# A HGRN2 mixer whose key products, sums and logarithms are placed anew on VectorE and ScalarE

## The chip, the cores and the metric

The kernel runs on one core of one Trainium2 chip. It computes one inference step of a small hybrid network (four layers; 512 noisy tokens and 128 context tokens) in one launch. The metric is the device time in microseconds, a median over runs. Engines are called TensorE (PE in the rows), VectorE (DVE), ScalarE (ACT), GpSimd (POOL) and SyncE (SP, which only starts DMAs here).

## The reference, cut to what matters

Four layers follow each other: differential attention, retention, HGRN2, differential attention. Each normalises its input, multiplies it with an input matrix, mixes the tokens, and multiplies with an output matrix. The change touches the HGRN2 layer alone. Its core, for each of 8 heads and for both directions:

```python
def gates(fl, lbd):
    f = lbd + (1.0 - lbd) * jax.nn.sigmoid(fl)
    return jnp.log(f), 1.0 - f                      # log decay g, key k

def step(S, inp):                                    # one chunk of 64 tokens
    qc, kc, vc, gc = inp
    b = lax.cumsum(gc, axis=1)
    ref = b[:, mid:mid + 1]
    sc = einsum(qc * exp(b - ref), kc * exp(ref - b)) * causal
    o = sc @ vc + (qc * exp(b)) @ S
    b_last = b[:, -1:]
    S = exp(b_last) * S + (kc * exp(b_last - b)).T @ vc
    return S, o

of, sf = gla_scan(q, kf, i, gf, s0[:, 0])
ob, sb = gla_scan(q[:, ::-1], kb[:, ::-1], i[:, ::-1], gb[:, ::-1], s0[:, 1])
o = rms_norm(of + ob[:, ::-1], norm_g)
y = (o * silu(g)) @ w_out
```

## The kernel before, in words

All tokens (640: 512 and 128) stand on the free axis; a head's 128 key channels are the partitions. Weights arrive in pieces of 512 KB. ScalarE copies each piece to a rounded type (`whi`, L178) and VectorE takes the rest (`wlo`, L116), so that three matmuls per product give full precision. A matmul group of the input projection is therefore three lines: L250 to L252 (one head's column of 128 outputs, 320 tokens at a time) or L225 to L227 (256 columns of values or of the output gate).

The HGRN2 layer (`hg`, L1056) first projects head 0 (`hg_proj`) and then, for each head h, weaves two generators: `hg_mix` of head h, the main one, and `hg_proj` of head h+1 as fill (for the last head the start of the output layer, `tail`). `hg_mix` yields numbers where TensorE would wait (6.0, 1.5, 6.0, 1.5, 4.0, 4.0), and `weave` issues as much fill as each number, scaled, asks for. This decides the order on TensorE, which is written by hand: it runs its instructions exactly in the order of issue. On the other engines the order is set by a scheduler, from the order of issue and its own estimate of times; there each engine too runs its queue strictly in order.

`hg_proj` of a head computes, in succession, a value or gate block (`iv` or `sg`, by the parity of the head; none for head 7), then three columns: the query `q`, the forward gate `th0`, the backward gate `th1`. Each column comes in two halves, and each half ends with a tanh on ScalarE (L1143). When a column is done, its weight buffers are handed to the next piece, so that a weight copy (L178) on ScalarE stands directly behind the column.

`hg_mix` does for each direction d: key `k` (VectorE), logarithm `g` (ScalarE, L1174, which needs another activation table than tanh and exp), running sum `c` (VectorE scan, L1177 or L1180), the difference `dd` to a reference, its exponentials `e1`, `e2` (L1186, L1187), the products `qd` (VectorE) and `kd` (GpSimd), the difference `xx` and its exponentials (L1197, L1198) with the half-size products `of` (two a direction), the exponential of `c` (L1204) with `qe` and `dl`, the distance `ll` to the block's end on GpSimd, its exponential (L1211), and the product `ke` on GpSimd. Then come four transposes of `ke` on TensorE (L1218), their copy `kt` on ScalarE (L1220), the state products (L1224), and VectorE's updates of the state (L1228). After both directions follow the score products (L1243 to L1247), masks, a sum on GpSimd (L1254), and the output products (L1259 to L1262). All products go through one helper line, L1155. The temporaries (`w0`, shown as `w`) rotate through five buffers.

Of the kernel before, what the change touches and what calls it, by code (L numbers as in the profile page):

```python
# [11 lines left out]
F32 = mybir.dt.float32  # L12
# [3 lines left out]
AF = mybir.ActivationFunctionType  # L16
ALU = mybir.AluOpType
# [4 lines left out]
P = 128  # L22
# [66 lines left out]
class Net:  # L89
# [966 lines left out]
    def hg(self, l, y):  # L1056
        nc, tc, t = self.nc, self.tc, self.t
        with tc.tile_pool(name=f"hg{l}", bufs=1, reuse_waits="tile") as mp:
            rs = self.const(mp, "rs")
            mf = mp.tile([P, NT, 64], U8, name="mf")  # L1060
            mg = mp.tile([P, NT, 64], U8, name="mg")
            for m, n in ((mf, "mf"), (mg, "mg")):
                c = mp.tile([P, 640], F32, tag="w0", bufs=5, name="w0")[:, 0:320]
                nc.sync.dma_start(c, t["consts"][:, CWHERE[n][0]:sum(CWHERE[n])])
                nc.vector.tensor_copy(m.rearrange("p a b -> p (a b)"), c)
            self.gain = self.gains[:, 0:1]

            tt_ = nc.vector.tensor_tensor
            mx = mp.tile([P, 2, 8], F32, name="lmx")
            ex = mp.tile([P, 2, 4, 8], F32, name="lex")  # L1070
            su = mp.tile([P, 2, 8], F32, name="lsu")
            tt_(out=mx, in0=self.lbl[:, :, 0, :], in1=self.lbl[:, :, 1, :], op=ALU.max)
            for i in (2, 3):
                tt_(out=mx, in0=mx, in1=self.lbl[:, :, i, :], op=ALU.max)
            tt_(out=ex, in0=self.lbl, in1=mx.unsqueeze(2).to_broadcast([P, 2, 4, 8]), op=ALU.subtract)
            nc.scalar.activation(ex, ex, AF.Exp)
            tt_(out=su, in0=ex[:, :, 0, :], in1=ex[:, :, 1, :], op=ALU.add)
            for i in (2, 3):
                tt_(out=su, in0=su, in1=ex[:, :, i, :], op=ALU.add)
            nc.vector.reciprocal(su, su)  # L1080
            tt_(out=ex, in0=ex, in1=su.unsqueeze(2).to_broadcast([P, 2, 4, 8]), op=ALU.mult)
            lb = mp.tile([P, 2, 8], F32, name="lb")
            tt_(out=lb, in0=ex[:, :, 0, :], in1=ex[:, :, 1, :], op=ALU.add)
            for i in range(2, l + 1):
                tt_(out=lb, in0=lb, in1=ex[:, :, i, :], op=ALU.add)
            tt_(out=lb, in0=lb, in1=ex[:, :, 0, :], op=ALU.subtract)
            co = mp.tile([P, 3, 2, 8], F32, name="lco")
            for i, (a, b) in enumerate(((-0.5, 0.5), (0.5, 0.5), (0.5, -0.5))):
                nc.vector.tensor_scalar(out=co[:, i], in0=lb, scalar1=a, scalar2=b, op0=ALU.mult, op1=ALU.add)
            pz = [mp.tile([P, NT, 64], F32, name=f"z{d}") for d in range(2)]  # L1090
            for z in pz:
                nc.vector.memset(z, 0.0)
            st = types.SimpleNamespace(mp=mp, l=l, rs=rs, mf=mf, mg=mg, co=co, pz=pz, iv={}, sg={}, h={})
            for _ in self.hg_proj(st, 0):
                pass
            for h in range(HEADS):
                if h < 7:
                    self.weave(self.hg_mix(st, h, y), self.hg_proj(st, h + 1), 24.0, 30.0 if h < 6 else 18.0)
                else:
                    self.weave(self.hg_mix(st, h, y), self.tail(l, y, 2), 24.0, 12.0)  # L1100

    def hg_proj(self, st, h):
        nc, t, mp = self.nc, self.t, st.mp
        if h == 0:
# [3 lines left out]
            def use(tt, ps):  # L1108
                nc.scalar.activation(iv[:, tt, :], ps[:, 0, :], AF.Copy)
                self.gate(sg[:, tt:tt + 1, :], ps[:, 1:2, :])  # L1110
# [11 lines left out]
        hd = st.h[h] = types.SimpleNamespace(th=[])  # L1122

        def halves(ps, j):
            return ((slice(j * 256, j * 256 + 256), samples(ps, j)), (slice(NS + j * 64, NS + j * 64 + 64), prompts(ps, j)))
# [11 lines left out]
        for d in range(2):  # L1137
            th = mp.tile([P, 640], F32, tag=f"th{d}", bufs=2, name="th")
            hd.th.append(th)

            def use(j, ps):
                for c, u in halves(ps, j):
                    nc.scalar.activation(th[:, c], u, AF.Tanh, scale=0.5)  # L1143

            yield from self.proj_b(st.l, 1024 + d * 1024 + h * 128, use)

    def hg_mix(self, st, h, y):
        nc, t, mp = self.nc, self.t, st.mp
        p, m = h // 2, h % 2
        iv, sg, rs, mf, mg, co, pz = st.iv[p], st.sg[p], st.rs, st.mf, st.mg, st.co, st.pz  # L1150
# [2 lines left out]
        ch = lambda a: a.rearrange("p (c i) -> p c i", i=64)  # L1153
        bl = lambda a: a.rearrange("p (c i) -> p c i", i=128)
        TT = lambda eng, o, a, b, op: eng.tensor_tensor(out=o, in0=a, in1=b, op=op)  # L1155
        DV, PL = nc.vector, nc.gpsimd

        def tmp():
            return mp.tile([P, 640], F32, tag="w0", bufs=5, name="w0")

        def lin(tag, n=640, bufs=1):
            return mp.tile([P, n], F32, tag=tag, bufs=bufs, name=tag)

        s32 = mp.tile([P, 8, P], F32, tag="s32", name="s32")
        for d in range(2):
            nc.sync.dma_start(s32[:, 4 * d, :], t["state_hgrn"][0, 0, d, h])
        res = []
        for d in range(2):
            th = st.h[h].th[d]
            hs, hb, nhs = (co[:, i, d, h:h + 1] for i in range(3))  # L1170
            k = lin(f"k{d}")
            DV.tensor_scalar(out=k, in0=th, scalar1=nhs, scalar2=hs, op0=ALU.mult, op1=ALU.add)
            g = tmp()
            nc.scalar.activation(g, th, AF.Ln, scale=hs, bias=hb)  # L1174
            c = lin(f"c{d}")
            if d == 0:
                DV.tensor_tensor_scan(c, rs, g, 0.0, op0=ALU.mult, op1=ALU.add)  # L1177
                ref, mid, last = 32, 63, 127
            else:
                DV.tensor_tensor_scan(c[:, ::-1], rs, g[:, ::-1], 0.0, op0=ALU.mult, op1=ALU.add)  # L1180
                ref, mid, last = 31, 64, 0

            dd = tmp()
            TT(DV, ch(dd), ch(c), ch(c)[:, :, ref:ref + 1].to_broadcast([P, 10, 64]), ALU.subtract)
            e1, e2 = tmp(), tmp()
            nc.scalar.activation(e1, dd, AF.Exp)  # L1186
            nc.scalar.activation(e2, dd, AF.Exp, scale=-1.0)  # L1187
            qd, kd = lin(f"qd{d}"), lin(f"kd{d}")
            TT(DV, qd, q, e1, ALU.mult)
            TT(PL, kd, k, e2, ALU.mult)  # L1190

            xx = tmp()
            TT(DV, bl(xx), bl(c), bl(c)[:, :, mid:mid + 1].to_broadcast([P, 5, P]), ALU.subtract)
# [12 lines left out]
            TT(DV, qe, q[:, 0:NS], ec_[:, 0:NS], ALU.mult)  # L1206
            dl = lin(f"dl{d}", 5)
            DV.tensor_copy(dl, bl(ec_)[:, :, last])
            ll = tmp()
            TT(PL, bl(ll), bl(c)[:, :, last:last + 1].to_broadcast([P, 5, P]), bl(c), ALU.subtract)  # L1210
            nc.scalar.activation(ll, ll, AF.Exp)  # L1211
            ke = tmp()
            TT(PL, ke, k, ll, ALU.mult)
            yield 6.0
            pt = self.one([P, 4, P])
            blocks = (0, 1, 2, 4) if d == 0 else (1, 2, 3, 4)
            for i, b in enumerate(blocks):
                nc.tensor.transpose(pt[:, i, :], bl(ke)[:, b, :], self.ident)  # L1218
            kt = mp.tile([P, 4, P], F32, tag=f"kt{d}", name="kt")
# [6 lines left out]
            for n, i in enumerate(order):  # L1226
                b = blocks[i]
# [21 lines left out]
        f2, g2 = pz  # L1249
        DV.copy_predicated(f2, mf, fd)  # L1250
        DV.copy_predicated(g2, mg, gp)
        p1 = bl(tmp())
        for s, u in ((A, B), (B, A)):
            TT(PL, p1[s, :, s], f2[s], g2[s], ALU.add)  # L1254
            nc.scalar.activation(p1[s, :, u], fo[s], AF.Copy)
        yield 4.0
        o = self.two([P, 8, P])
# [180 lines left out]
```

## Time and profile before

| | |
|---|---|
| median of 3 runs | 1885.02 us (1884.73 to 1887.43) |
| the profiled execution's own time | 1885.44 us |
| its span | 1883.7 us |
| busy: TensorE, weight load, VectorE, ScalarE, GpSimd | 96%, 88%, 69%, 52%, 16% |
| mean granted TensorE clock | 0.989 of full speed |
| the HGRN2 heads | about 1086 to 1420 us of the span |

The span is the time between the first and last recorded instruction; the device time lies 1.7 us above it. A busy share of TensorE is an average over four layers. The heads of the HGRN2 layer follow each other at about 43 us: the forward logarithms of heads 0, 3 and 7 start at 1087.9, 1216.2 and 1380.8 us.

### The profile page before, as it was taken

The numbers are of one execution on the slowest core, as the hardware profiler recorded it, in microseconds if no ns is written. First come the engines' busy times: TensorE is split into PE (matmuls) and PEld (weight loads), VectorE is DVE, ScalarE is ACT, GpSimd is POOL, SyncE is SP. The second block draws the span as 40 slices with busy tenths as digits, with TensorE's granted clock in tenths as the row PEclk, the third lists the DMA queues.
The fourth block names the chain that finished last, engine by engine and source line by source line (L and its number), as shares of the span: only waits on it lengthen the run. The fifth ranks groups of instructions, "written<-read, shape, count | busy, mean of one in ns | idle before, by whom it ended". The sixth has DMA issues, their size and how long they took to land.

```text
span 1883.7 us, 31931 instructions
## 1 busy us (share of the span) xinstructions
PE 1804.6 (96%) x12060; PEld 1650.3 (88%) x12060; DVE 1304.6 (69%) x2681; ACT 980.7 (52%) x2271; POOL 300.2 (16%) x249
## 2 busy tenths in 40 slices
PE   5999999999999999999999999999989999999998
PEld 3889999977888889889878899999978889999976
DVE  4878888847788898873335566666774776767654
ACT  3556676655544434443333366666664545655552
POOL 0000000003222223222101222332331200000001
PEclk9999999999999999999999999999989999999999
DMA  9644555414454445343323222222214463443322
GB/s 302 187 127 139 148 151 167 119 49 154 122 164 149 135 151 157 124 135 101 116 92 101 86 69 74 65 63 74 62 41 137 139 170 90 114 115 101 98 73 101
DMA packets 231536, 224.39 MB, mean 119 GB/s; under 512 B 11619, under 2 KB 201558, under 8 KB 231382
## 3 DMA queue, kind: packets, MB, share of 16 engines
q1 hardware_dynamic: 230912, 221.96, 39.3%
q8 instruction: 95, 1.56, 0.3%
q14 instruction: 59, 0.48, 0.1%
q10 hardware_dynamic: 470, 0.39, 0.1%
HBM read 174.59 MB, written 18.35 MB: 102 GB/s over the span
## 4 chain that ended last, share of the span: by engine, by line
PE 66%; DVE 15%; ACT 7%; DMA 5%; issue 3%; SPq 2%; POOL 1%; DVEq 0%; ACTq 0%; POOLq 0%
PE one L470 7%; PE one L472 7%; PE one L471 7%; PE one L250 5%; PE one L251 5%; PE one L252 5%; PE one L225 3%; PE one L826 3%; PE one L226 3%; PE one L227 3%; DVE macc L367 3%; DVE wlo L116 2%; PE two L788 2%; PE two L789 2%; PE one L816 1%
## 5 line engine op out<-in xcount | busy, mean ns | idle before, releaser
L250 PE MATMUL one<-hh,whi 128*128 128x320 f32 x1152 | 364.8, 317 | 3.9 <-DVE modT L339 1.6
L252 PE MATMUL one<-hh,wlo 128*128 128x320 f32 x1152 | 356.4, 309 | 0.3 <-DVE wlo L116 0.3
L251 PE MATMUL one<-hl,whi 128*128 128x320 f32 x1152 | 356.4, 309 | 0.0
L116 DVE TENSOR_TENSOR wlo<-raw,whi 128x1024 fp32r<-128x1024 f32 x192 | 235.9, 1234 | 143.9 <-ACT whi L178 143.2
L470 PE MATMUL one<-whi,hh 128*128 128x512 f32 x744 | 301.8, 406 | 6.8 <-ACT yo L565 3.5
L472 PE MATMUL one<-whi,hl 128*128 128x512 f32 x744 | 294.6, 396 | 0.4 <-DVE hl L444 0.4
L471 PE MATMUL one<-wlo,hh 128*128 128x512 f32 x744 | 292.9, 394 | 0.0
L178 ACT ACTIVATE whi<-raw 128x1024 fp32r<-128x1024 f32 x192 | 201.5, 1056 | 152.8 <-PE one L251 58.6
L250 PEld LDWEIGHTS one<-hh,whi 128*128 128x128 f32 x1152 | 217.3, 189 | 6.0 <-DVE modT L339 2.0
L251 PEld LDWEIGHTS one<-hl,whi 128*128 128x128 f32 x1152 | 217.4, 189 | 0.5
L252 PEld LDWEIGHTS one<-hh,wlo 128*128 128x128 f32 x1152 | 217.2, 189 | 0.5 <-DVE wlo L116 0.5
L367 DVE SCALAR_TENSOR_TENSOR macc<-mraw,smod,macc 128x256 f32<-128x256 f32 x432 | 209.1, 527 | 1.3 <-DMA mraw<-in_w_mod 1.1
L397 POOL TENSOR_TENSOR rs<-ms,mhalf 128x1 f32<-128x1 f32 (+1 forms) x72 | 65.7, 913 | 897.6 <-DVE ms L395 724.4
L225 PE MATMUL one<-whi,hh 128*128 128x256 f32 x720 | 207.7, 289 | 0.0
L226 PE MATMUL one<-wlo,hh 128*128 128x256 f32 x720 | 201.0, 279 | 0.0
L227 PE MATMUL one<-whi,hl 128*128 128x256 f32 x720 | 200.9, 279 | 0.0
L470 PEld LDWEIGHTS one<-whi,hh 128*128 128x128 f32 x744 | 141.6, 190 | 37.2 <-ACT yo L565 3.9
L472 PEld LDWEIGHTS one<-whi,hl 128*128 128x128 f32 x744 | 141.0, 190 | 34.5 <-DVE hl L444 1.3
L471 PEld LDWEIGHTS one<-wlo,hh 128*128 128x128 f32 x744 | 141.5, 190 | 27.7
L225 PEld LDWEIGHTS one<-whi,hh 128*128 128x128 f32 x720 | 135.4, 188 | 1.5
L226 PEld LDWEIGHTS one<-wlo,hh 128*128 128x128 f32 x720 | 135.6, 188 | 0.0
L227 PEld LDWEIGHTS one<-whi,hl 128*128 128x128 f32 x720 | 135.1, 188 | 0.0
(345 smaller groups left out, 3540.1 us busy)
## 6 DMA issues: line engine op xcount, KB each, us to landing
mraw<-in_w_mod SPq DMA_DIRECT2D x96, 512.0 KB, 4.1
raw<-in_da_w_in SPq DMA_DIRECT2D x56, 512.0 KB, 4.5
raw<-in_hg_w_in SPq DMA_DIRECT2D x36, 512.0 KB, 3.9
raw<-in_ret_w_in SPq DMA_DIRECT2D x64, 256.0 KB, 3.0
kk<-ks SPq DMA_DIRECT2D x64, 160.0 KB, 2.9
kz<-ks SPq DMA_DIRECT2D x64, 160.0 KB, 2.8
qq<-q SPq DMA_DIRECT2D x64, 128.0 KB, 3.0
raw<-in_da_w_out SPq DMA_DIRECT2D x16, 512.0 KB, 3.9
```

The lines of the kernel that those rows point to most:

```text
L116: return (eng or self.nc.gpsimd).tensor_tensor(out=out, in0=full, in1=hi.bitcast(F32), op=ALU.subtract)
L178: self.nc.scalar.activation(hi, raw, AF.Copy)
L225: mm(out, xh, wh[:, k % 4, :], start=(first and k == ks[0]), stop=False)
L226: mm(out, xh, wl[:, k % 4, :], start=False, stop=False)
L227: mm(out, xl, wh[:, k % 4, :], start=False, stop=(last and k == ks[-1]))
L250: nc.tensor.matmul(ps, wh[:, k, :], self.hh[:, k, c], start=(k == 0), stop=False)
L251: nc.tensor.matmul(ps, wh[:, k, :], self.hl[:, k, c], start=False, stop=False)
L252: nc.tensor.matmul(ps, wl[:, k, :], self.hh[:, k, c], start=False, stop=(k == KT - 1))
L367: nc.vector.scalar_tensor_tensor(out=m, in0=raw[:, k, :], scalar=c, in1=m, op0=ALU.mult, op1=ALU.add)
L470: mm(ps, xh, wh, start=(first and k == ks[0]), stop=False)
L471: mm(ps, xh, wl, start=False, stop=False)
L472: mm(ps, xl, wh, start=False, stop=(last and k == ks[-1]))
```

## The change

Five edits, all in `hg_mix` but for one handle:
- both directions' logarithms are issued in succession, and made to stand behind the last tanh of the head's projection (`issue_after`);
- `kd`, `ke` and the sums of L1254 move from GpSimd to VectorE;
- the distance `ll` is no longer computed: the exponential takes `c` with scale -1 and the block's last value as its bias, one instruction for each of the four blocks that are needed;
- the product `ke` is made for the needed blocks alone (384 + 128 columns forward, 512 backward);
- the temporaries rotate through six buffers (also where the masks are loaded, L1063).

```diff
@@ hg_proj
-                    nc.scalar.activation(th[:, c], u, AF.Tanh, scale=0.5)
+                    hd.last = nc.scalar.activation(th[:, c], u, AF.Tanh, scale=0.5)
@@ hg_mix
-            return mp.tile([P, 640], F32, tag="w0", bufs=5, name="w0")
+            return mp.tile([P, 640], F32, tag="w0", bufs=6, name="w0")
-        res = []
+        res, gs = [], [tmp(), tmp()]
+        with self.tc.issue_after(st.h[h].last.ins):
+            for d in range(2):
+                nc.scalar.activation(gs[d], st.h[h].th[d], AF.Ln, scale=co[:, 0, d, h:h + 1], bias=co[:, 1, d, h:h + 1])
         for d in range(2):
-            th = st.h[h].th[d]
-            hs, hb, nhs = (co[:, i, d, h:h + 1] for i in range(3))
+            th, g = st.h[h].th[d], gs[d]
+            hs, nhs = co[:, 0, d, h:h + 1], co[:, 2, d, h:h + 1]
-            g = tmp()
-            nc.scalar.activation(g, th, AF.Ln, scale=hs, bias=hb)
...
-            TT(PL, kd, k, e2, ALU.mult)
+            TT(DV, kd, k, e2, ALU.mult)
...
-            ll = tmp()
-            TT(PL, bl(ll), bl(c)[:, :, last:last + 1].to_broadcast([P, 5, P]), bl(c), ALU.subtract)
-            nc.scalar.activation(ll, ll, AF.Exp)
+            blocks = (0, 1, 2, 4) if d == 0 else (1, 2, 3, 4)
             ke = tmp()
-            TT(PL, ke, k, ll, ALU.mult)
+            for b in blocks:
+                nc.scalar.activation(bl(ke)[:, b, :], bl(c)[:, b, :], AF.Exp, scale=-1.0, bias=bl(c)[:, b, last:last + 1])
+            for bs in (slice(0, 3), slice(4, 5)) if d == 0 else (slice(1, 5),):
+                TT(DV, bl(ke)[:, bs, :], bl(ke)[:, bs, :], bl(k)[:, bs, :], ALU.mult)
...
-            TT(PL, p1[s, :, s], f2[s], g2[s], ALU.add)
+            TT(DV, p1[s, :, s], f2[s], g2[s], ALU.add)
```

On TensorE and on SyncE the instructions and their order are the same before and after (line numbers behind the edits are one higher). GpSimd keeps one small instruction a head in this layer. ScalarE and VectorE are ordered anew.

ScalarE before, head 3, from the forward gate's last tanh on (`th` are the gates, `w` with a number a temporary, `hsq` the squares of head 2's output):

```order
L178 ACTIVATE whi<-raw 128x1024
L1143 ACTIVATE th<-one 128x256
L1143 ACTIVATE th<-one 128x64
L1174 ACT_TABLE_LOAD
L1174 ACTIVATE w_13052<-th,lco 128x640
L1143 ACT_TABLE_LOAD
L1143 ACTIVATE th<-one 128x256
L1143 ACTIVATE th<-one 128x64
L1186 ACTIVATE w_13058<-w_13056 128x640
L1187 ACTIVATE w_13059<-w_13056 128x640
```

And the same place after, where the `th` rows are the backward gate's two halves:

```order
L1143 ACTIVATE th<-one 128x256
L1143 ACTIVATE th<-one 128x64
L649 ACTIVATE hsq,hss<-two 128x128 x5
L178 ACTIVATE whi<-raw 128x1024
L1143 ACTIVATE th<-one 128x256
L1143 ACTIVATE th<-one 128x64
L1170 ACT_TABLE_LOAD
L1170 ACTIVATE w_13059<-th,lco 128x640
L1170 ACTIVATE w_13060<-th,lco 128x640
L1187 ACT_TABLE_LOAD
L1187 ACTIVATE w_13069<-w_13067 128x640
L1188 ACTIVATE w_13070<-w_13067 128x640
```

The forward logarithm stood behind the forward gate, with the backward gate's tanh behind it; now both logarithms stand behind the backward gate's second half, with one table load ahead of them and one behind.

VectorE before, head 3, from the forward scan on (`c` the running sum, the two `w` the differences `dd` and `xx`; the forward `ke` was GpSimd's):

```order
L1177 SCALAR_TENSOR_TENSOR c_13054<-c_rs,w_13052 128x640
L1155 TENSOR_TENSOR w_13056<-c_13054 128x640
L1155 TENSOR_TENSOR w_13066<-c_13054 128x640
L1155 TENSOR_TENSOR qd_13062<-q,w_13058 128x640
L1155 TENSOR_TENSOR of_13071<-k_13050,w_13068 128x5x64
L1155 TENSOR_TENSOR of_13071<-q,w_13068 128x5x64
L1155 TENSOR_TENSOR qe_13076<-q,w_13074 128x512
L1208 COPY dl_13078<-w_13074 128x5
```

And after, from the forward scan to the forward `ke` (`w_13091`, the last row of its two):

```order
L1178 SCALAR_TENSOR_TENSOR c_13065<-c_rs,w_13059 128x640
L1181 SCALAR_TENSOR_TENSOR c_13219<-c_rs,w_13060 128x640
L1155 TENSOR_TENSOR w_13067<-c_13065 128x640
L1155 TENSOR_TENSOR w_13077<-c_13065 128x640
L1155 TENSOR_TENSOR qd_13073<-q,w_13069 128x640
L1155 TENSOR_TENSOR kd_13074<-k_13063,w_13070 128x640
L1155 TENSOR_TENSOR w_13221<-c_13219 128x640
L632 SCALAR_TENSOR_TENSOR sg<-sg,one 128x512
L1155 TENSOR_TENSOR of_13082<-k_13063,w_13079 128x5x64
L1155 TENSOR_TENSOR qe_13087<-q,w_13085 128x512
L1155 TENSOR_TENSOR w_13091<-w_13091,k_13063 128x384
L1155 TENSOR_TENSOR w_13091<-w_13091,k_13063 128x128
```

Ahead of the forward `ke` now stand the other direction's scan and difference, `kd`, and the `ke` products themselves. In heads 0, 2 and 4 there is no `sg` row here; the backward direction's second difference stands ahead of `ke` in its place.

## Rows read from the trace of the kernel before

**Rows 1.** Busy by stretch: length, PE, PEld, DVE, ACT, POOL, granted PE clock, DMA, GB/s.
```profile
1085.00:1130.00 45.00, 43.39 (x372) 42.98 (x371) 29.31 (x38) 28.56 (x49) 11.17 (x8) 1.00 0.21 63
...
1210.00:1250.00 40.00, 39.89 (x355) 39.50 (x354) 28.03 (x42) 26.27 (x51) 10.87 (x7) 1.00 0.20 58
...
1330.00:1370.00 40.00, 36.72 (x308) 36.00 (x307) 27.10 (x45) 26.11 (x55) 12.98 (x9) 1.00 0.23 67
1370.00:1420.00 50.00, 42.93 (x348) 38.63 (x347) 31.19 (x52) 29.93 (x63) 14.01 (x11) 0.83 0.12 37
...
1370.00:1372.00 2.00, 2.00 (x10) 2.00 (x9) 0.59 (x2) 0.60 (x1) 0.00 (x0) 0.50 0.56 202
1372.00:1374.00 2.00, 2.00 (x13) 2.00 (x12) 0.00 (x0) 0.00 (x0) 0.00 (x0) 0.65 0.00 0
```

**Rows 2.** What TensorE waited for in the heads: total us, times, longest.
```profile
PE one L1224 <- ACT kt L1220: 2.8, 2, 1.6
...
PE one L1218 <- POOL w L1155: 2.1, 1, 2.1
```

**Rows 3.** TensorE's timeline, heads 3 and 6: start us, us, line, op, tiles.
```profile
1213.38 0.31 PE L250 MATMUL one<-hh,whi 128*128 128x320 f32 x1
...
1223.32 0.28 PE L225 MATMUL one<-whi,hh 128*128 128x256 f32 x1
...
1231.80 0.60 PE L1218 MATMUL one<-c_ident,w 128*128 128x128 f32 x4
...
1352.92 0.31 PE L250 MATMUL one<-hh,whi 128*128 128x320 f32 x1
...
1358.20 0.60 PE L1218 MATMUL one<-c_ident,w 128*128 128x128 f32 x4
```

**Rows 4.** ScalarE's timeline, head 3, behind the forward gate's column.
```profile
1213.43 1.06 ACT L178 ACTIVATE whi<-raw 128x1024 fp32r<-128x1024 f32 x1 [2.88 <-PE one L251]
...
1216.19 0.93 ACT L1174 ACTIVATE w<-th,lco 128x640 f32<-128x640 f32 x1
```

**Rows 5.** VectorE's timeline, head 3.
```profile
1217.15 1.49 DVE L1177 TENSOR_TENSOR_SCAN c<-c_rs,w 128x640 f32<-128x640 f32 x1 [0.87 <-ACT w L1174]
1218.67 1.56 DVE L1155 TENSOR_TENSOR w<-c 128x640 f32<-128x640 f32 x2
1220.36 0.82 DVE L1155 TENSOR_TENSOR qd<-q,w 128x640 f32<-128x640 f32 x1
...
1232.55 0.68 DVE L632 SCALAR_TENSOR_TENSOR sg<-sg,one 128x512 f32<-128x512 f32 x1
1233.15 0.82 DVE L1155 TENSOR_TENSOR qd<-q,w 128x640 f32<-128x640 f32 x1
```

**Rows 6.** Instructions on temporaries, all heads: ns min/median/max, first and last start.
```profile
L1155 POOL TENSOR_TENSOR kd<-k,w x16: 1552/1578/2027, 1092.7 to 1401.7; 128x640 f32<-128x640 f32 x16
...
L1197 ACT ACTIVATE w<-w x16: 455/472/473, 1092.5 to 1402.1; 128x320 f32<-128x320 f32 x16
...
L1155 DVE TENSOR_TENSOR of<-k,w x16: 869/1520/1870, 1093.0 to 1402.9; 128x320 f32<-128x320 f32 x16
L1204 ACT ACTIVATE w<-c x16: 721/724/731, 1093.2 to 1403.3; 128x640 f32<-128x640 f32 x16
...
L1155 DVE TENSOR_TENSOR qe<-q,w x16: 676/679/1428, 1096.0 to 1405.1; 128x512 f32<-128x512 f32 x16
```

**Rows 7.** TensorE's and VectorE's timeline, head 7, with the output layer's pieces.
```profile
1387.02 1.25 PE L460 MATMUL one<-c_ident,y 128*128 128x128 f32 x10
...
1394.11 1.79 DVE L444 SCALAR_TENSOR_TENSOR hl<-one,par,hh 128x512 fp32r<-128x512 f32 x3
1395.82 1.48 DVE L1180 TENSOR_TENSOR_SCAN c<-c_rs,w 128x640 f32<-128x640 f32 x1
...
1400.03 1.06 PE L1218 MATMUL one<-c_ident,w 128*128 128x128 f32 x4
...
1401.16 0.81 DVE L1155 TENSOR_TENSOR qd<-q,w 128x640 f32<-128x640 f32 x1
```

More of the change, by code (lines that the diff above doesn't have):

```diff
@@ L1062, in hg @@
             for m, n in ((mf, "mf"), (mg, "mg")):
-                c = mp.tile([P, 640], F32, tag="w0", bufs=5, name="w0")[:, 0:320]
+                c = mp.tile([P, 640], F32, tag="w0", bufs=6, name="w0")[:, 0:320]
                 nc.sync.dma_start(c, t["consts"][:, CWHERE[n][0]:sum(CWHERE[n])])
@@ L1155, in hg_mix @@
         TT = lambda eng, o, a, b, op: eng.tensor_tensor(out=o, in0=a, in1=b, op=op)
-        DV, PL = nc.vector, nc.gpsimd
+        DV = nc.vector
         def tmp():
-            return mp.tile([P, 640], F32, tag="w0", bufs=5, name="w0")
+            return mp.tile([P, 640], F32, tag="w0", bufs=6, name="w0")
         def lin(tag, n=640, bufs=1):
@@ L1208, in hg_mix @@
             DV.tensor_copy(dl, bl(ec_)[:, :, last])
-            ll = tmp()
-            TT(PL, bl(ll), bl(c)[:, :, last:last + 1].to_broadcast([P, 5, P]), bl(c), ALU.subtract)
-            nc.scalar.activation(ll, ll, AF.Exp)
+            blocks = (0, 1, 2, 4) if d == 0 else (1, 2, 3, 4)
             ke = tmp()
-            TT(PL, ke, k, ll, ALU.mult)
+            for b in blocks:
+                nc.scalar.activation(bl(ke)[:, b, :], bl(c)[:, b, :], AF.Exp, scale=-1.0, bias=bl(c)[:, b, last:last + 1])
+            for bs in (slice(0, 3), slice(4, 5)) if d == 0 else (slice(1, 5),):
+                TT(DV, bl(ke)[:, bs, :], bl(ke)[:, bs, :], bl(k)[:, bs, :], ALU.mult)
             yield 6.0
             pt = self.one([P, 4, P])
-            blocks = (0, 1, 2, 4) if d == 0 else (1, 2, 3, 4)
             for i, b in enumerate(blocks):
```

## Prediction

> **What bounds the kernel now.** I read the busy times by stretch first, since a share over the whole span mixes four layers. In the HGRN2 layer TensorE is busy 39.9 of 40 us around head 3, 36.7 of 40 around head 6, and 42.9 of 50 around head 7, there at a granted clock of 0.83 [rows 1]. Up to head 5, then, TensorE's own instruction stream sets the time: work taken off another engine gives nothing, and a wait added to TensorE is paid in full. Besides 1.6 us in head 0, only heads 6 and 7 have idle time to win. The table of waits says what ends the idle time of TensorE inside the heads: 2.8 us for `kt` (1.6 in head 0, 1.2 in head 6) and 2.1 us for the key products `w` of GpSimd, in head 6 [rows 2].
>
> So the view that decides is TensorE's timeline of one head, read for the place where the mixer's first result is wanted. In head 3 the last projection column that the mixer needs (the backward gate, second half) ends at 1223.32; TensorE then runs other heads' projection until 1231.80, where the four transposes of the forward `ke` stand (L1218) [rows 3]. The fill between them is 8.48 us, and nothing of it can move: TensorE's order is written by hand, and is the same before and after the change.
>
> **What the change moves.** Before, the forward direction does not start from 1223.32 but from the end of the *previous* column, the forward gate: 1213.38 [rows 3]. Right behind it ScalarE cuts a weight piece (1213.43), runs the last tanh of that column, loads the table and takes the logarithm (1216.19), and VectorE's scan starts at 1217.15 [rows 4, 5], 3.77 us after the column. So `ke` had 18.4 us (1213.38 to 1231.80) before TensorE asked for it, and was there in time.
>
> After it, ScalarE takes both logarithms behind the last tanh of the backward gate, which needs the column that ends at 1223.32. Weight piece, tanh, table load and first logarithm now stand behind this column in the same sequence, so I carry the 3.77 us over: the forward scan starts at about 1227.1. From there I add what the new order puts on VectorE up to the forward `ke`:
> - two scans of 1.49 us each, the second for the other direction: 2.9 with a little overlap [rows 5];
> - the two subtractions up to the start of `qd`: 1.69 (1218.67 to 1220.36) [rows 5];
> - `qd`, `kd` (new here, from GpSimd) and the other direction's subtraction, 640 wide each: 0.82 less the 0.08 by which such instructions overlap (the `sg` piece of 0.68 starts at 1232.55, the next at 1233.15), 0.74 each: 2.2 [rows 5];
> - in heads 1, 3 and 5 a gate piece `sg`, 0.60; in heads 0, 2 and 4 another subtraction stands ahead of `ke` in its stead, 0.74 [rows 5];
> - the two half-size products `of`: see below, 0.76 together;
> - `qe` (0.68) and the tiny `dl`, with overlap: 0.7 [rows 6];
> - the two new products for `ke`, 384 and 128 wide: 0.6, an estimate on the same line as `of`.
>
> Together 9.5 us, so `ke` is ready 3.8 + 9.5 = 13.3 us after the column, and TensorE wants it 8.5 us after. TensorE stands for **4.8 us** in each of heads 0 to 5. Everything behind that is later by as much and finds its inputs: the mixer asks for as much fill again before the second transposes, and for the backward `ke` VectorE has only a subtraction, `qd`, `kd`, `of`, `qe` and one product left, some 4.5 us.
>
> ScalarE could be later than VectorE: behind the first exponential it has one of full size (0.72), two halves (0.47 each), one more of full size and the four new ones, whose bias is the block end's logarithm. For these no row stands. Below, the four together cost the 0.72 of the one that goes; above, four times 0.47, a row with 320 columns against their 128 [rows 6]. By the upper end ScalarE needs 4.3 us and VectorE 4.3 to 4.5 us from the same point, so VectorE sets it, and at worst the gate piece adds 0.5. I take VectorE's sum.
>
> The price of `of` is the uncertain one. In the trace before it takes 1.52 us for 320 columns, while `qe` takes 0.68 for 512 and `qd` 0.82 for 640 [rows 5, 6]; the line through the two gives 0.46. GpSimd's `kd` (1.58) [rows 6] runs beside `of` in each head. After the change GpSimd has none of the products, so I take 0.46, less overlap; if GpSimd is not what stretches it, `of` stays at 1.52, and 2 x 1.06 us come on top in each of eight heads. The shortest `of`, 0.87, lies between the two [rows 6]. The Trainium skill ("SBUF — State Buffer", section "Who interferes with whom") states that a VectorE instruction with two inputs in SBUF and a GpSimd instruction that reads SBUF exclude each other for a whole instruction. By that rule the lower price and the sum hold; the trace agrees as far as its shortest `of` goes.
>
> What leaves at no gain: GpSimd's four products and sums a head, and two table loads of ScalarE a head. Their cover is TensorE's stream in heads 0 to 5. What comes at no cost: the two sums of L1254 on VectorE, since TensorE has fill up to the output products; and a wait that the buffers add. With six of them the backward exponential of `c` takes the buffer of the forward `ke`, so ScalarE waits there for TensorE's transposes, and in heads 0 and 4 `kt` is queued behind it and behind the four new exponentials, at most 0.7 + 1.9 us. The fill between transposes and state products hides that; without it TensorE would wait up to 2.6 us in two heads.
>
> **The sum, by heads.**
> - Heads 0 to 5: 6 x 4.8 = 28.8, less head 0's own wait of 1.6 [rows 2]: +27.2.
> - The clock. After the wait of 2.1 us in head 6 the granted clock was 0.50 over 1370 to 1372 and 0.65 over 1372 to 1374 [rows 1]: 1.0 + 0.7 = 1.7 us of TensorE's work lost, the lower of its two levels (1.2 against 2.4 GHz). The new waits are over twice as long, so I take one such stretch in each of the six heads: +10.2. Bounds: nothing, if the slow stretch falls into the wait itself; two stretches, 20.4.
> - Head 6: the fill is shorter, from 1352.92 to 1358.20, 5.28 us [rows 3], and neither `sg` nor the extra subtraction stands ahead: 13.3 - 0.6 - 5.3 = 7.4 us of waiting. It takes the place of 1.2 + 2.1 [rows 2] and of a slow stretch that is there before and after: +4.1.
> - Head 7: its column ends at 1387.02 and the transposes start at 1400.03 [rows 7]; here pieces of the output layer (L443, L444) share ScalarE and VectorE. Scan at about 1391.4 (3.8 behind the column, and 0.6 for the squarings of head 6's output, which end behind it here), 1.5 for it, 1.7 for three pieces (1394.11 to 1395.82): the other scan at 1394.6 and no longer at 1395.82, so `qd`, at 1401.16 before, comes 1.2 earlier [rows 7]. But that `qd` is now the forward one, and behind it stand `kd`, the subtraction (0.74 each with `qd`), one piece (0.7), `of`, `qe` and `ke`, 5.0 in all, before the forward `ke` is there, at 1405.0: **+5.0**, where it was ready long ahead before.
>
> 27.2 + 10.2 + 4.1 + 5.0 = 46.5 us on the profiled execution's 1885.4, which lies 0.4 above the median of the runs shown: **1932 us**, 2.5% slower.
>
> **Rivals.**
> - *The clock is kept* (chance 0.13): the waits come as said, but TensorE is back at the full level when it goes on. For it: after head 0's 1.6 us the clock of its stretch is 1.00 [rows 1]; against: after 2.1 us there is. 1922.
> - *VectorE is not relieved* (0.09): `of` stays at 1.5. For it: the trace never shows `of` with GpSimd idle throughout. 46.5 + 8 x 2.1: 1949.
> - *The relief decides, faster* (0.04): the forward `ke` still arrives before TensorE asks. Then the waits of heads 0 and 6 go (1.6 + 3.3), with them the slow stretch (1.7) and some 1.2 in head 7, where VectorE is earlier: 1877. It decides only if the chain from column to `ke` fits into 8.5 us; the trace has 3.8 before the scan and two scans of 1.5 already, so 1.7 would have to hold all that follows. Heads 6 and 7 are what speaks for it.
> - *Nothing moves* (0.03): the chain is hidden in some way I do not see, and heads 6 and 7 trade waits: 1885.
>
> **How the numbers follow.** The forecast itself has 0.71. Its own bounds (stall 4.3 to 5.5 a head, clock loss 0 to two stretches) give 1919 to 1946; with the rivals beside it the range is 1912 to 1950. Of this kernel a difference of 0.2%, 3.8 us, can be told from none. Slower by more than that: 0.71 + 0.13 + 0.09 = 0.93; within it 0.03; faster 0.04.
>
> **What would show it.** TensorE's table of waits should name L1219 (the transposes, now one line on) waiting for VectorE's `w` in seven or eight heads, 4.3 to 5.5 us each in heads 0 to 5 and over 7 in head 6, and head 0's wait for `kt` should be gone. `of` should read near 0.46. The granted clock should show a slow stretch behind each wait. I am wrong if TensorE's idle time in heads 1 to 5 stays near zero, or if the wait stands at another line, `kt` or the score products.

## The result and the profile after

The changed kernel takes **1931.45 us** (median, 1930.77 to 1932.37); runs of the kernel before beside it have a median of 1885.72 us. The ratio is 1.0248 with a 95% interval of 1.0236 to 1.026: 2.5% slower, 0.6 us from the forecast of 1932. The profiled execution has a span of 1929.7 us against 1883.7, so 46.0 us have to be found.

TensorE's table of waits in the heads of this layer (line waited for and releaser: us in total, times, longest) holds most of them:

```profile
PE one L1219 <- DVE w L1155: 42.2, 8, 7.4
PE one L460 <- DVE hl L444: 5.6, 3, 4.3
...
PE one L460 <- ACT th L1143: 0.5, 1, 0.5
```

TensorE waits at the forward transposes in all eight heads, for VectorE's product `ke`. The waits for `kt` and for GpSimd's `w` [rows 2] are gone. Before, these heads held 11.9 us of such waits (4.9 of [rows 2], and 7.0 at the output layer's pieces, L460); after, 42.2 + 5.6 + 0.5 = 48.3. That is 36.4 of the 46.0 us. The two rows of L460 in the kernel before:

```profile
PE one L460 <- DVE hl L444: 4.4, 3, 3.3
...
PE one L460 <- ACT th L1143: 2.6, 1, 2.6
```

TensorE's timeline shows them one by one (start, duration, line, tiles, in brackets the idle time just before): heads 0, 1, 3, 5, 6 and 7.

```profile
1102.76 1.09 PE L1219 MATMUL one<-c_ident,w 128*128 128x128 f32 x4 [4.69 <-DVE w L1155]
...
1152.87 1.08 PE L1219 MATMUL one<-c_ident,w 128*128 128x128 f32 x4 [4.83 <-DVE w L1155]
...
1238.88 0.28 PE L225 MATMUL one<-whi,hh 128*128 128x256 f32 x1
...
1252.03 1.09 PE L1219 MATMUL one<-c_ident,w 128*128 128x128 f32 x4 [4.52 <-DVE w L1155]
...
1351.08 1.09 PE L1219 MATMUL one<-c_ident,w 128*128 128x128 f32 x4 [4.83 <-DVE w L1155]
...
1399.74 1.08 PE L1219 MATMUL one<-c_ident,w 128*128 128x128 f32 x4 [7.41 <-DVE w L1155]
...
1443.59 1.09 PE L1219 MATMUL one<-c_ident,w 128*128 128x128 f32 x4 [5.96 <-DVE w L1155]
```

Heads 0 to 5 wait 28.8 us together (4.5 to 5.0 each), head 6 waits 7.4, head 7 6.0. The row of 1238.88 is the place of head 3 where the backward gate's column ends (before: 1223.32 [rows 3]). TensorE arrives at the transposes at 1252.03 - 4.52 = 1247.51, 8.6 us behind the column, and `ke` comes 13.2 us behind it. The chain from the column to `ke`, on ScalarE and VectorE, reads:

```profile
1238.93 1.06 ACT L178 ACTIVATE whi<-raw 128x1024 fp32r<-128x1024 f32 x1 [1.41 <-PE one L251]
...
1241.69 1.74 ACT L1170 ACTIVATE w<-th,lco 128x640 f32<-128x640 f32 x2
...
1242.65 1.49 DVE L1178 TENSOR_TENSOR_SCAN c<-c_rs,w 128x640 f32<-128x640 f32 x1 [0.53 <-ACT w L1170]
1244.06 1.47 DVE L1181 TENSOR_TENSOR_SCAN c<-c_rs,w 128x640 f32<-128x640 f32 x1
...
1247.05 0.82 DVE L1155 TENSOR_TENSOR qd<-q,w 128x640 f32<-128x640 f32 x1
...
1249.86 0.48 DVE L1155 TENSOR_TENSOR of<-k,w 128x320 f32<-128x320 f32 x1
...
1251.34 0.75 DVE L1155 TENSOR_TENSOR w<-w,k 128x384 f32<-128x384 f32 x2
```

Column at 1238.88, both logarithms in one pass, the forward scan at 1242.65 (3.77 us behind the column, as [rows 3, 5] had it behind the *earlier* column), the backward scan right behind it, and from there VectorE without a gap up to `ke`. The instructions on the temporaries over all heads (ns, min/median/max) give two of the prices:

```profile
L1213 ACT ACTIVATE w<-c x64: 386/388/392, 1100.0 to 1447.2; 128x128 f32<-128x128 f32 x64
...
L1155 DVE TENSOR_TENSOR of<-k,w x16: 477/484/487, 1099.8 to 1445.8; 128x320 f32<-128x320 f32 x16
```

`of` fell from 1520 to 484 ns [rows 6]; one new exponential costs 388 ns. The busy times by stretch (columns as in [rows 1]) show what the waits left of TensorE and of its clock:

```profile
1180.00:1230.00 50.00, 45.03 (x376) 44.67 (x375) 26.78 (x49) 25.64 (x59) 1.17 (x1) 0.93 0.20 59
1230.00:1280.00 50.00, 45.48 (x383) 45.12 (x383) 29.44 (x53) 26.24 (x61) 1.17 (x1) 0.97 0.20 59
...
1101.00:1105.00 4.00, 2.24 (x11) 2.27 (x12) 4.00 (x9) 4.00 (x11) 0.00 (x0) 0.55 0.00 0
```

Where TensorE was busy 39.89 of 40 us at a granted clock of 1.00 [rows 1], it is busy 45 of 50 at 0.93 and 0.97. The last row is the end of head 0's wait and what follows: of 4 us TensorE is idle 1.76, and the clock is 0.55, near the lower level (1.2 of 2.4 GHz). GpSimd is down to one instruction in 50 us.

### The profile page after: what moved, and what is told of

Read it like the earlier page. It is cut to its first block, busy times and chain, and to the rows that moved or that the text cites. A ratio compares the mean times of both kernels' runs of the same rounds, so it can differ in the third digit from the quotient of the medians.

```text
span 1929.7 us, 31893 instructions
## 1 busy us (share of the span) xinstructions
PE 1813.7 (94%) x12060; PEld 1659.5 (86%) x12060; DVE 1298.4 (67%) x2737; ACT 967.8 (50%) x2303; POOL 209.3 (11%) x185
## 4 chain that ended last, share of the span: by engine, by line
PE 73%; DVE 13%; ACT 5%; DMA 4%; issue 2%; SPq 2%; POOL 1%; DVEq 0%; ACTq 0%; POOLq 0%
PE one L470 8%; PE one L472 7%; PE one L471 7%; PE one L250 7%; PE one L251 7%; PE one L252 6%; PE one L225 4%; PE one L226 3%; PE one L227 3%; PE one L826 3%; DVE macc L367 2%; PE two L788 2%; PE two L789 2%; PE one L816 1%; DVE wlo L116 1%
## 5 line engine op out<-in xcount | busy, mean ns | idle before, releaser
L225 PE MATMUL one<-whi,hh 128*128 128x256 f32 x720 | 212.6, 295 | 0.0
L226 PE MATMUL one<-wlo,hh 128*128 128x256 f32 x720 | 205.0, 285 | 0.0
L470 PEld LDWEIGHTS one<-whi,hh 128*128 128x128 f32 x744 | 141.2, 190 | 37.5 <-ACT yo L565 4.3
L472 PEld LDWEIGHTS one<-whi,hl 128*128 128x128 f32 x744 | 140.5, 189 | 34.4 <-DVE hl L444 1.3
L471 PEld LDWEIGHTS one<-wlo,hh 128*128 128x128 f32 x744 | 141.1, 190 | 27.5
L225 PEld LDWEIGHTS one<-whi,hh 128*128 128x128 f32 x720 | 140.6, 195 | 1.5
L226 PEld LDWEIGHTS one<-wlo,hh 128*128 128x128 f32 x720 | 140.4, 195 | 0.0
L227 PEld LDWEIGHTS one<-whi,hl 128*128 128x128 f32 x720 | 139.6, 194 | 0.0
```

Source lines behind the costliest of these rows:

```text
L225: mm(out, xh, wh[:, k % 4, :], start=(first and k == ks[0]), stop=False)
L226: mm(out, xh, wl[:, k % 4, :], start=False, stop=False)
L227: mm(out, xl, wh[:, k % 4, :], start=False, stop=(last and k == ks[-1]))
L470: mm(ps, xh, wh, start=(first and k == ks[0]), stop=False)
L471: mm(ps, xh, wl, start=False, stop=False)
L472: mm(ps, xl, wh, start=False, stop=(last and k == ks[-1]))
```

## The experiments

Each ratio is to the kernel before as it ran beside that experiment (medians of 1884.3 to 1886.1 us), so a difference of medians between two experiments is loose by 1 to 2 us.

**One part undone: the logarithms.** The changed kernel with the logarithms alone put back where they were. Edit:

```diff
-        res, gs = [], [tmp(), tmp()]
-        with self.tc.issue_after(st.h[h].last.ins):
-            for d in range(2): nc.scalar.activation(gs[d], st.h[h].th[d], AF.Ln, ...)
+        res = []
...
+            g = tmp()
+            nc.scalar.activation(g, th, AF.Ln, scale=hs, bias=hb)
```

> The changed kernel with only the logarithms put back (each direction's logarithm in its own turn, the forward one behind the forward gate's tanh); products and sums stay on VectorE, the bias of the exponential and the six buffers stay. Theory: the place of the logarithms is the whole loss, so TensorE's waits for the forward key products go in all eight heads, and what is left is a gain on the kernel before: head 6's wait for the backward key products (2.1 us) and the slow stretch behind it (1.7) go, head 0's wait for kt stays or moves to heads 0, 2 and 4 at about 1 us. 1878 to 1885. Rival: the products on VectorE and the four small exponentials carry part of the loss: 1890 to 1905, with waits of 1 us or more a head for w on VectorE.

Measured: 1890.59 us (1887.51 to 1894.41), ratio to before 1.0032 (1.0019 to 1.0044). So 41 of the 46 us are the logarithms' place. But I had expected it to be faster than before (1878 to 1885 us), and it is 0.3% slower, at the lower end of the rival's range. The rival's waits for VectorE's `w` are not there; the four small exponentials do cost, but at another place. Its table of waits names it:

```profile
PE one L1224 <- ACT kt L1220: 8.2, 6, 1.6
```

And ScalarE's and TensorE's timelines of head 3 show it:

```profile
1233.68 0.97 ACT L1212 ACTIVATE w<-c 128x128 f32<-128x128 f32 x3
...
1234.56 0.57 ACT L1220 ACTIVATE kt<-one 128x512 f32<-128x512 f32 x1
...
1235.19 1.16 PE L1224 MATMUL one<-iv,kt 128*128 128x128 f32 x8 [1.15 <-ACT kt L1220]
```

`kt`, which brings the forward transposes out of PSUM, stands on ScalarE behind three or four of the *backward* direction's small exponentials. These wait for nothing but the backward `c`, so they are put ahead of it; the single exponential of the kernel before waited for GpSimd's subtraction and so stood behind (head 3 before: `kt` at 1234.70, that exponential at 1236.89). TensorE pays 1.2 to 1.6 us in each of heads 0 to 5. Head 6 gives nothing back either, though I had expected it to: where the kernel before waited 2.1 us for GpSimd's product, TensorE now waits 2.9 us at the second transposes for VectorE's `q` of the next head (L1133).

**One part alone: the logarithms.** The kernel before with the logarithms in succession and six buffers, nothing else:

```diff
-            return mp.tile([P, 640], F32, tag="w0", bufs=5, name="w0")
+            return mp.tile([P, 640], F32, tag="w0", bufs=6, name="w0")
...
+        with self.tc.issue_after(st.h[h].last.ins):
+            for d in range(2): nc.scalar.activation(gs[d], st.h[h].th[d], AF.Ln, ...)
```

> The kernel before with only the logarithms in succession behind the last tanh (and the six buffers they need); products, sums and the distance to the block's end stay on GpSimd. Theory: the chain behind the late logarithms is then longer, since GpSimd does kd, the distance and ke one after the other at 1.5 to 1.6 us each: the forward ke about 14.4 us behind the column, 5.9 us of waiting a head where the changed kernel has 4.8. 1936 to 1950, slower than the changed kernel. Rival: the late logarithms alone are hidden, and the loss is the work that VectorE took over: 1885 to 1895.

Measured: 1945.46 us (1943.34 to 1950.59), ratio 1.033 (1.0309 to 1.0351). TensorE's waits:

```profile
PE one L1219 <- POOL w L1155: 57.4, 8, 9.0
```

The same place, eight times, now for GpSimd's `ke`. The time is in my range, but the waits are longer than I had them: 5.7 to 7.3 us in heads 0 to 5, against a forecast of 5.9. This part alone costs more than the whole change; the other parts together (products and sums on VectorE, the exponentials with a bias) give some 14 us of it back.

**One part alone: products and sums on VectorE.** The kernel before, with this only:

```diff
-            TT(PL, kd, k, e2, ALU.mult)
+            TT(DV, kd, k, e2, ALU.mult)
...
-            TT(PL, ke, k, ll, ALU.mult)
+            TT(DV, ke, k, ll, ALU.mult)
...
-            TT(PL, p1[s, :, s], f2[s], g2[s], ALU.add)
+            TT(DV, p1[s, :, s], f2[s], g2[s], ALU.add)
```

> The kernel before with only the products and sums on VectorE (kd, ke, the two sums); logarithms as before, the distance still on GpSimd with one exponential. Theory: hidden behind TensorE in heads 0 to 5; only heads 6 and 7 can gain. 1879 to 1887. Rival: VectorE, now with some 4 us more a head, gets late: 1890 or more, with waits for VectorE's w in heads 1 to 5.

Measured: 1878.78 us (1873.99 to 1882.95), ratio 0.9969 (0.9958 to 0.998): 0.3% faster, and 0.2 us below my range. That only heads 6 and 7 could gain does not hold; the last point on the prediction says where the rest lies. GpSimd's and VectorE's timelines of head 3 also settle what stretches `of`:

```profile
1230.43 1.57 POOL L1155 TENSOR_TENSOR w<-c 128x640 f32<-128x640 f32 x1 [6.97 <-ACT w L1198]
...
1230.81 1.54 DVE L1155 TENSOR_TENSOR of<-k,w 128x320 f32<-128x320 f32 x1
1232.28 0.48 DVE L1155 TENSOR_TENSOR of<-q,w 128x320 f32<-128x320 f32 x1
```

Of two equal products, the one beside GpSimd's remaining subtraction takes 1.54 us and the next, with GpSimd idle, 0.48. It is so throughout: of the 32 `of` of the layer, 14 begin with 1.2 us of such a subtraction still to run, take 1.54 to 1.55 us and end 0.34 to 0.36 us behind it; the other 18 take 0.48 to 0.49, among them four that begin just ahead of a subtraction.

**The clock by itself.** The changed kernel, with 28 matmuls that compute nothing needed ahead of the forward transposes of heads 0 to 5, so that TensorE works while it would wait:

```diff
+            if d == 0 and h < 6:
+                junk = pt.rearrange("p a b -> p (a b)")[:, 0:320]
+                for _ in range(28):
+                    nc.tensor.matmul(junk, self.hh[:, 0, 0:128], self.hh[:, 0, 0:320], start=True, stop=True)
```

> The changed kernel, with 28 matmuls of no use (128x320, into the buffer of the transposes, overwritten by them) ahead of the forward transposes of heads 0 to 5, where TensorE stood 4.5 to 5.0 us: 28 x 0.147 = 4.1 us of work in the place of idle time. Theory: the waits themselves stay (the key products are no earlier), but the granted clock stays at the full level behind them, so the 9.6 us that the waits of the two traces leave over (46.0 less 36.4 more idle time) come back: 1919 to 1925. Rival: the 9.6 us are no matter of the clock (or the clock falls whatever TensorE does there): 1929 to 1936; if the extra matmuls were late themselves, up to 1955.

Measured: 1920.17 us (1917.66 to 1924.8), ratio 1.0196 (1.0171 to 1.022). Its waits at the transposes:

```profile
PE one L1223 <- DVE w L1155: 17.3, 8, 7.4
```

And its busy times over heads 2 and 3 (columns as in [rows 1]):

```profile
1180.00:1230.00 50.00, 49.23 (x421) 48.77 (x421) 26.79 (x49) 27.39 (x67) 1.17 (x1) 1.00 0.21 61
1230.00:1280.00 50.00, 49.36 (x422) 48.91 (x422) 29.16 (x56) 26.76 (x61) 2.34 (x2) 1.00 0.20 59
```

The filling is too short to outlast a wait (0.5 to 0.8 us is left in each head), so `ke` is as late as in the changed kernel; only the clock is different, 1.00 throughout. What it gains, 11.3 us by the medians and 9.8 by the two ratios, is therefore the clock's price in these six heads, 1.6 to 1.9 us a head.

**More fill.** The changed kernel, with TensorE's order written anew: 3.3 us more of other heads' projection between the column and the forward transposes.

```diff
-            yield 6.0
+            yield 8.5 if d == 0 else 6.0
...
-        yield 4.0
+        yield 4.5
```

> The changed kernel, with TensorE's order rewritten so that about 3.3 us more of other heads' projection lies between the backward gate's column and the forward transposes (the mixer asks for 8.5 of fill there instead of 6.0, and for 4.5 instead of 4.0 ahead of the output products). Theory (the loss is a shortage of fill: the key product arrives 13.2 us after the column, TensorE asks 8.5 us after): the waits of heads 1 to 5 (24.1 us) go to near zero and with them their slow stretches, head 0 keeps under 1 us, head 6 about 2.3 instead of 7.4, head 7 stays: 1885 to 1893 us. Rival (TensorE's order only shifts the wait to the second transposes, the score products or the output products, because the chain of VectorE and ScalarE is the longer one in a head): the idle time of the heads stays near 40 us under other lines, 1915 to 1932.

Measured: 1914.55 us (1911.56 to 1916.74), ratio 1.016 (1.014 to 1.018); 22 us above the upper end of my range and just below the rival's 1915. Its waits:

```profile
PE one L1225 <- ACT kt L1221: 17.2, 7, 3.0
...
PE one L1219 <- DVE w L1155: 4.9, 2, 4.4
```

ScalarE's timeline of head 3, up to `kt`:

```profile
1250.71 0.72 ACT L1205 ACTIVATE w<-c 128x640 f32<-128x640 f32 x1
1251.34 1.27 ACT L1213 ACTIVATE w<-c 128x128 f32<-128x128 f32 x4
1252.51 1.04 ACT L178 ACTIVATE whi<-raw 128x1024 fp32r<-128x1024 f32 x1
1253.46 0.57 ACT L1221 ACTIVATE kt<-one 128x512 f32<-128x512 f32 x1
```

The wait at the transposes left as the theory says: in heads 1 to 5 nothing of 24.1 us is left, 0.45 in head 0 and 4.4 in head 6. But 2.2 to 3.0 us a head took its place one step later, at `kt`, which is queued behind the backward direction's exponential of `c`, its four small ones and a weight piece. So the rival was right that the wait moves to another line, and wrong about which: it named neither the state products nor `kt`.

**`kt` first, with that fill.** The last kernel, with those exponentials put behind `kt` (the weight piece stays ahead):

```diff
+            if d == 0:
+                nc.scalar.activation(ec_, c, AF.Exp)
+            else:
+                with self.tc.issue_after(kti.ins):
+                    nc.scalar.activation(ec_, c, AF.Exp)
...
-            nc.scalar.activation(kt, pt, AF.Copy)
+            kti = nc.scalar.activation(kt, pt, AF.Copy)
```

> The kernel with more fill ahead of the forward transposes (1914.6 us), with the eviction kt of the forward transposes put on ScalarE ahead of the backward direction's exponential of c and its four small ones; TensorE's order is the same, and one weight piece (1.0 us) still stands ahead of kt. Theory (with the fill the shortage at the forward transposes is gone, and what is left in heads 0 to 5 is kt, behind 0.7 + 1.3 us of backward exponentials and the weight piece): the waits at the state products fall from 17.2 us in all to 6 to 9 (1.0 to 1.4 a head), most of the slow stretches behind them go: 1892 to 1903 us. Rival (the weight piece ahead of kt waits for TensorE, so kt is no earlier; or the backward key product, later by 0.6 us, becomes late): a wait of 2 us or more stays in each head, 1908 to 1916 us.

Measured: 1895.21 us (1890.82 to 1897.4), ratio 1.0049 (1.0032 to 1.0067), with

```profile
PE one L1229 <- ACT kt L1225: 6.8, 7, 1.6
```

As expected. With the logarithms still in succession, 36 of the 46 us are won back: 17 by fill (1931.5 to 1914.6), 19 by the place of `kt` (to 1895.2; 21 by the ratios).

**The forward direction first.** The changed kernel, with the backward scan kept off VectorE until the forward `ke` is done:

```diff
-                DV.tensor_tensor_scan(c[:, ::-1], rs, g[:, ::-1], 0.0, op0=ALU.mult, op1=ALU.add)
+                with self.tc.issue_after(kei.ins):
+                    DV.tensor_tensor_scan(c[:, ::-1], rs, g[:, ::-1], 0.0, op0=ALU.mult, op1=ALU.add)
...
-                TT(DV, bl(ke)[:, bs, :], bl(ke)[:, bs, :], bl(k)[:, bs, :], ALU.mult)
+                kei = TT(DV, bl(ke)[:, bs, :], bl(ke)[:, bs, :], bl(k)[:, bs, :], ALU.mult)
```

> The changed kernel, both logarithms still in succession behind the backward gate, but the backward scan issued on VectorE only behind the forward key product, so that the forward chain holds no backward work. Theory (of the 4.8 us a head, the scan of 1.4 and a subtraction of 0.74, in even heads two, are the other direction's; the rest is the later column): the forward key product arrives some 10.8 us after the column, TensorE waits 2.2 to 2.8 us instead of 4.5 to 5.0 in heads 0 to 5, the waits at the forward transposes sum to 18 to 22 us instead of 42.2: 1908 to 1916 us. Rival 1 (ScalarE's exponentials set the end, not VectorE's order): waits stay at 4 us and above, 1926 to 1932. Rival 2 (the backward half is now late instead): new waits at the second transposes or the score products, 1920 to 1935.

Measured: 1910.21 us (1903.85 to 1911.05), ratio 1.0127 (1.0103 to 1.0151). Its waits at the transposes:

```profile
PE one L1220 <- DVE w L1155: 28.2, 8, 6.4
```

VectorE's timeline of head 3, the forward `ke` and now behind it the backward scan:

```profile
1242.76 0.75 DVE L1155 TENSOR_TENSOR w<-w,k 128x384 f32<-128x384 f32 x2
1243.43 1.48 DVE L1182 TENSOR_TENSOR_SCAN c<-c_rs,w 128x640 f32<-128x640 f32 x1
```

And the busy times over heads 2 and 3:

```profile
1180.00:1230.00 50.00, 47.36 (x414) 47.00 (x413) 26.92 (x49) 27.06 (x66) 1.17 (x1) 1.00 0.24 70
1230.00:1280.00 50.00, 47.15 (x396) 46.79 (x395) 28.88 (x55) 27.18 (x65) 2.33 (x2) 0.97 0.21 61
```

The waits of heads 0 to 5 fall to 2.4 to 2.9 us each: about 2.1 of the 4.8 us a head were the other direction's work in VectorE's queue, the rest is the later column. The waits sum to 28.2 us, where I had expected 18 to 22: I had put heads 6 and 7 too low (5.7 and 6.4, head 7 not better at all). The time is inside my range all the same, because two errors cancel: the waits fell by less, but what they leave over in the span fell too, from 9.6 to 4.5 us, and my range held only the waits. No new wait at the second transposes or the score products came.

**`kt` first, without the logarithms.** The first of these kernels, with the four backward exponentials behind `kt`; nothing else moves:

```diff
+            if d == 0:
+                for b in blocks: near(b)
+            else:
+                with self.tc.issue_after(kti.ins):
+                    for b in blocks: near(b)
...
-            nc.scalar.activation(kt, pt, AF.Copy)
+            kti = nc.scalar.activation(kt, pt, AF.Copy)
```

Here `near(b)` is the exponential of block b.

> The kernel with the logarithms back in the loop, and on ScalarE the eviction kt of the forward transposes put ahead of the backward direction's four small exponentials instead of behind them; nothing else moves on any engine. Theory (its 0.3% over the kernel before is kt standing behind 1.0 to 1.3 us of small exponentials, while TensorE waits 8.2 us at the state products in six heads and 1.7 us in head 7): these waits fall under 2 us in all, 1878 to 1884 us, level with the kernel that only moves the products. Rival (the four small exponentials cost ScalarE 0.5 us a direction more than the single one wherever they stand, and the backward key product is now late): a wait at the second transposes takes their place, 1887 to 1891.

Measured: 1883.67 us (1878.32 to 1888.87), ratio 0.9996 (0.9984 to 1.0009). Its table of waits has

```profile
PE one L470 <- ACT kt L1228: 1.7, 1, 1.7
PE one L1232 <- ACT kt L1228: 1.2, 4, 0.4
```

The 8.2 us in six heads are down to 1.2, and the time falls by 0.36%. Head 7's 1.7 stay, so the waits for `kt` are 2.9 in all and not under 2. It is level with the kernel before, but not with the products alone (ratio 0.9969), so the exponentials with a bias (here with six buffers) do not pay even there. The traces of one execution each show where the difference lies. From the forward transposes of head 0 to those of head 5 this kernel takes 216.8 us (1095.93 to 1312.76) and the products alone 213.5 (1100.23 to 1313.69). About half of that is again `kt`: from the transposes to the state products 3.55 to 3.79 us a head, against 3.27 there (3.62 in head 0). The other half is the longer of the two times of one block of matmuls that the last section tells of. Heads 6 and 7 add another 3.2 us.

**The distance on VectorE.** The products-only kernel, with the subtraction taken off GpSimd too and the single exponential kept:

```diff
-            TT(PL, bl(ll), bl(c)[:, :, last:last + 1].to_broadcast([P, 5, P]), bl(c), ALU.subtract)
+            TT(DV, bl(ll), bl(c)[:, :, last:last + 1].to_broadcast([P, 5, P]), bl(c), ALU.subtract)
```

> The kernel before with key products and sums on VectorE, and the distance to the block's end subtracted on VectorE too instead of on GpSimd, with the single full-size exponential: the same relief of GpSimd as in the changed kernel, without the bias. Theory (TensorE is busy throughout in heads 1 to 5 already, so nothing there can be won): level with the kernel that leaves the subtraction on GpSimd, 1876 to 1881 us; of at 0.48 us in both halves, against 1.54 in the half that now meets the subtraction. Rival (VectorE, with 0.74 us more a direction, makes the forward key product late): waits at the forward transposes in heads 0 to 6, 1885 to 1895.

Measured: 1875.78 us (1873.39 to 1877.77), ratio 0.9955 (0.9938 to 0.9971): the lowest median of all, ahead of both kernels of this case, though its interval overlaps that of the products alone. It is 0.2 us below my range. Its `of` over all heads, first half:

```profile
L1155 DVE TENSOR_TENSOR of<-k,w x16: 481/485/490, 1093.4 to 1394.9; 128x320 f32<-128x320 f32 x16
```

And what is left of TensorE's waits in the heads, the largest three that this layer's work has a part in:

```profile
PE one L460 <- DVE hl L444: 2.8, 3, 1.6
PE one L460 <- ACT th L1143: 2.4, 1, 2.4
PE one L1218 <- DVE w L1155: 2.3, 2, 1.8
```

With GpSimd idle beside them, these sixteen `of` take 0.48 to 0.49 us, and VectorE's extra 0.74 us a direction costs TensorE nothing before head 6.

## Why the prediction was right

- *What bounds the heads.* Right: TensorE's stream, and `ke` at L1219. The table of waits names the line and releaser that were forecast.
- *The chain from the column.* Forecast 3.8 + 9.5 = 13.3 us, measured 13.2 in head 3, against a fill of 8.6 (forecast 8.5). The 4.8 us a head, 28.8 in six heads, came to 28.8. The kernel with the backward scan held back splits them: about 2.1 queue, 2.7 column.
- *Head 6 and head 7.* In head 6 7.4 forecast, 7.41 measured. In head 7 I forecast 5.0 at the transposes and nothing else; TensorE waits 5.96 there and loses 0.95 less at the output layer's pieces than before (7.07 to 6.12). That the sum is +5.0 is luck: two errors of 1 us cancel. All waits together were forecast at 36.3 (27.2 + 4.1 + 5.0) and came to 36.4.
- *The clock.* Forecast 10.2. Span less idle leaves 46.0 - 36.4 = 9.6 over all heads, the filled kernel shows 9.8 to 11.3 in heads 0 to 5. TensorE's timeline gives it head by head: from the forward transposes to the state products, with the same matmuls between and no recorded wait, it takes 5.6 to 5.8 us in heads 0, 2 and 4 and 4.6 to 4.7 in heads 1, 3 and 5, against 3.5 before (without head 0's wait), some 10 us more in all. The size was right, the picture too simple: the stretch at the lower level is not the same in each head (granted clock 0.93 over one head's 50 us and 0.97 over the next), and it begins while TensorE still waits, as the row of head 0 shows (0.55 over 4 us of which 1.76 are idle) and head 2 more plainly (0.60 over 1200 to 1202, all of it wait), so only part of it is paid. The rival of a clock that is kept (1922) fell; the filled kernel, at 1920, is what it would have been.
- *`of`.* Forecast 0.46, measured 0.484; the rival in which VectorE is not relieved (1949) fell. The products-only kernel shows the cause, 1.54 beside GpSimd and 0.48 behind it in the same head. The rule of the Trainium skill ("SBUF — State Buffer", section "Who interferes with whom"), that such instructions of the two engines shut each other out, agrees: an `of` that begins beside GpSimd's subtraction ends 0.35 us behind it, at 1232.35 against 1232.00 in the rows above.
- *The new exponentials.* 0.388 us each, 1.27 for four: inside the bounds of 0.72 to 1.9. VectorE set the end, not ScalarE, as taken: in head 3 the last of the four ends at 1250.63 and VectorE comes to `ke` at 1251.34.
- *`kt` behind the buffers.* I put the queue ahead of `kt` at up to 2.6 us in heads 0 and 4, by a wait for a buffer, and let fill hide it. In the changed kernel it is hidden, but the mechanism was another. No wait for a buffer shows. In heads 0, 2 and 4 the backward exponentials run ahead of `kt` while TensorE's transposes are late by the stall, so they cost `kt` only 1 us (head 0: transposes done at 1103.85, `kt` at 1104.90, the state products at 1108.55). In heads 1, 3 and 5 `kt` stands ahead of them (head 3: `kt` at 1253.16, the backward exponential of `c` at 1254.38). Where the stall was taken away (more fill, or the logarithms put back) `kt` was late in six heads, by 2.2 to 3.0 and by 1.2 to 1.6 us. This is the step that I had too small, in two heads and for another reason, and it is why two of my expectations missed.
- *No gain in heads 1 to 5 from relief.* Nearly right: the products alone gain 0.3%. In the two profiled executions the stretch from head 0's forward transposes to the first row of L509, where the last head ends, is 7.2 us shorter (314.8 to 307.5): 3.1 us of it in heads 6 and 7, 1.4 in head 0's wait for `kt`, and the rest in heads 1 to 5, some 0.5 to 0.6 a head. The rows of heads 2 and 3 say how.

```profile
1185.89 0.60 PE L1218 MATMUL one<-c_ident,w 128*128 128x128 f32 x4
...
1220.33 0.28 PE L225 MATMUL one<-whi,hh 128*128 128x256 f32 x1
...
1228.49 0.60 PE L1218 MATMUL one<-c_ident,w 128*128 128x128 f32 x4
...
1231.76 1.05 PE L1224 MATMUL one<-iv,kt 128*128 128x128 f32 x8
```

And in the kernel before, beside the transposes at 1231.80 [rows 3]:

```profile
1188.62 0.60 PE L1218 MATMUL one<-c_ident,w 128*128 128x128 f32 x4
...
1235.33 0.94 PE L1224 MATMUL one<-iv,kt 128*128 128x128 f32 x6
```

From one head's forward transposes to the next are 42.60 us here; in the kernel before 43.18 (1188.62 to 1231.80). About half of the 0.58 us is `kt`: from the transposes to the state products TensorE needs 3.27 us here (1228.49 to 1231.76) and needed 3.53 before (1231.80 to 1235.33), with the same matmuls between; before, `kt` ends only at 1235.27. The other half is told at the end.

## What to carry over

Ask of every merged or regrouped step which *input* the earliest of its results now waits for: two table loads saved on an engine that waits anyway cost 41 us, because the direction that was wanted first now had to wait for the column of the one that was wanted last. Measure the fill between an input's last matmul and the consumer's place in TensorE's order, and add up the new chain against it, instruction by instruction; here that gave the loss to within 1 us, with two errors in head 7 that cancelled. When such a stall is removed, look next at what it was hiding: instructions that become ready early are put ahead of the one that TensorE asks for next.

## What was not expected of the hardware

- The same 72 matmuls of 256 columns take 8.16 us in head 3 of the products-only kernel (1220.33 to 1228.49) and 8.48 in the kernel before (1223.32 to 1231.80 [rows 3]), without a gap and with the granted clock at 1.00 in both: 113 or 118 ns from one to the next. In the kernel before all of heads 0 to 5 take the longer time, in the products-only kernel head 0 alone, in the changed kernel heads 0 and 3. What selects the one or the other stays open; it is worth 0.3 us a head.
- TensorE's clock answers to waits unevenly. After waits of 2.4 to 2.9 us (the kernel with the forward direction first) one 50-us stretch keeps 1.00 and the next has 0.97; after 4.5 to 5.0 us, 0.93 and 0.97. Nor does the longer wait get the longer slow stretch: after 4.69 us in head 0 of the changed kernel TensorE takes 5.79 us from the transposes to the state products, after 4.83 in head 1 only 4.74.
